# One mixer's value and output-gate products in another order, with their raw weight blocks asked for earlier

## The chip, the core and the metric

The kernel runs on one core of a Trainium2 chip. Its time is the device time of one execution in microseconds (us), the median of several. TensorE (PE) multiplies, VectorE (DVE) and ScalarE (ACT) work element by element, GpSimd (POOL) does a few element-wise pieces and issues the transfers that add what they bring to what is there (accumulating transfers), SyncE (SP) issues the plain loads. Each engine works through its own queue in order: an instruction that waits holds up what stands behind it on that engine.

## What is computed

Two layers of a decoder trunk on 512 tokens of width 1024, in fp32. Each layer is a mixer and a squared-ReLU MLP. The mixer:

```python
h = rmsnorm(x, norm_mix)
z = h @ w_in
splits = [int(s) for s in np.cumsum(IN_WIDTHS)[:-1]]
q_a, k_a, v_a, q_m, k_m, v_m, o_m, if_m, gates = jnp.split(z, splits, axis=-1)
...
att = sliding_window_attention(q_a, k_a, v_a, att_sinks)
...
hm = mlstm_chunkwise(...)
hm = rmsnorm(hm, m_head_norm.reshape(M_HEADS, M_V_DIM)).reshape(B, S, M_V_W)
hm = hm * jax.nn.sigmoid(o_m)
g_a, g_m = jnp.split(gates, 2, axis=-1)
mixed = jax.nn.sigmoid(g_a) * (att @ w_att_branch) + jax.nn.sigmoid(g_m) * (hm @ w_m_branch)
x = x + mixed @ w_out
```

The change concerns the columns `v_m` (values) and `o_m` (output gate) of `h @ w_in`, 512 columns each.

## The kernel before

**Matmuls.** Every fp32 operand is split into a high part (`wh`, a rounded copy made by ACT) and a low part (`wl`, the difference, made by DVE), and every product of tiles is three matmuls of 128x128 by 128x512 (`mm3`). A weight block of 128x512 (256 KB) comes by a plain load from SP into one of three raw buffers, is split into one of four pairs of `wh` and `wl` (`chunk`), and PE uses it for a fixed number of steps. Product banks in PSUM come from five in rotation.

**Order.** `weave` lays a list of PE steps (`fill`, each with a width) in a row and puts the pieces of a second list (`side`) between them where the running width passes their number. So a number such as 24.5 in `side` is a place in the row of PE steps. In one mixer that row is: the mLSTM's q and k (0 to 8), the gates `s0` (8 to 16), the gates `s1`, here called the second gates (16 to 24), product 2 (24 to 26), the two attention projections `a_steps` (26 to 34), the other six products (34 to 46), the gates `s2` and `s3` (46 to 62). Attention's pieces lie in `side` up to about 24, the mLSTM's from 39.6 on.

**Seven products instead of eight.** The tokens are cut in two halves, and so are the 1024 rows of the weights; with the two column groups (output gate and values) there would be eight products of half by half. The kernel computes seven, Strassen's scheme, from sums of weight blocks and sums of token halves. `plan` names for each product the held pair of PSUM banks ("x", "y" or "f"), the half of the activations if no sum is needed, and what is read from the banks at its end: `output` (gate) or `value`. A product in the list `fresh` takes new banks, another one adds onto what its pair holds. Each product has four weight blocks k and two token blocks i, eight steps of one `mm3`; `by_weights` goes through them block by block, `by_tokens` takes two weight blocks for one token block and then for the other.

**Raw blocks.** Products 1 and 2 use plain blocks through `chunk`. The others use `wa[k]` (5, 6, 4) and `wb[k]` (3, 7), each split by `parts_of` (ACT L722, DVE L723): `begin` loads a block by SP (L713) and has POOL add a second one to it (L729); `begin_other` loads `wb[k]`; after the split of product 5, 6 or 3, `more` (L717) has POOL add the block that turns it into the next product's weights. That addition must wait for the split and must land before the next split. The sums of tokens are made by DVE in `sums1`, `sums_next` and `sums3` into a scratch (`sc`), and split (L175, L176).

**What is read at the ends.** `output` copies a bank to SBUF (ACT) the first time and adds to it (DVE L795) the second time; `gates_o` then takes four tanh at 49.1. `value` writes the values `vm`, the first time by ACT (L786), then by DVE (L788). `m_gate` multiplies a head of the mLSTM's output by its gate. `qk_split` splits the mLSTM's q and k, with small copies on POOL (CAST, L676) and low parts on DVE (L679, L682).

Of the kernel before, what the change touches and what calls it, by code (L numbers as in the profile page):

```python
# [16 lines left out]
P = 128  # L17
# [16 lines left out]
def hybrid_kernel(ctx, tc, x, norm_mix, w_in, att_q_norm, att_k_norm, att_sinks, m_gate_bias,  # L34
# [353 lines left out]
    def mixer(l, norm, late, order, phase):  # L388
# [156 lines left out]
        qT, sps, parts = {}, {}, {}  # L545
# [76 lines left out]
        def att_probs(b, kv):  # L622
            sp = sps[b, kv]
            pt = aux()
            for i in range(4):
                pe.transpose(pt[:, i * P:(i + 1) * P], sp[:, i * P:(i + 1) * P], ident)
            hl = split(pt, get=lambda: temp(F32R))
            parts[b, kv] = [(hl, v2[:, 0, max(b - 1, 0), kv])]
            if b > 0:


                own = [temp(F32R) for _ in hl]
                for src, dst in zip(hl, own):
                    s3, d3 = (t.rearrange("p (h q) -> p h q", h=4) for t in (src, dst))
                    gp.affine_select(out=d3, in_=s3, compare_op=ALU.is_ge, fill=0.0, base=0,
                                     pattern=[[0, 4], [1, P]], channel_multiplier=-1)
                parts[b, kv].append((own, v2[:, 1, b - 1, kv]))
# [88 lines left out]
        def begin(k):  # L726
            wa[k] = slot()
            load(wa[k], 0, 0, k)
            gp.dma_start(wa[k], block(0, 1, k), accum_op=ALU.add)  # L729
# [60 lines left out]
        def output(t, i, ps, first):  # L790
            if first:
                so.append(slot() if t else temp())
                sc.activation(so[-1], ps, AF.Copy)
            else:
                ve.tensor_tensor(so[2 * t + i], so[2 * t + i], ps, op=ALU.add)  # L795
# [86 lines left out]
        def m_out(h, t):  # L882
# [11 lines left out]
            if h > 1:  # L894
                m_gate(h, t)

        def m_gate(h, t):
            c = slice(h * MV, (h + 1) * MV)
            ve.scalar_tensor_tensor(hm[t][:, c], so[t][:, c], 1.0, hm[t][:, c], op0=ALU.add, op1=ALU.mult)
# [10 lines left out]

        def a_steps(g, sg):
            def ev_a(m, ps):
                t = sg[m]
                prod.append(t)
                ve.scalar_tensor_tensor(t, t, 1.0, ps, op0=ALU.add, op1=ALU.mult)  # L915

            return feat_steps(att_acts, lambda k: [w_att_branch[l, k * P:(k + 1) * P, 512 * g:512 * g + 512]],
                              ev_a)
# [3 lines left out]
        side += [(27.0, sums1), (31.0, lambda: sums_next(6, 0, 0)), (33.5, lambda: sums_next(3, 0, 1)), (38.0, sums3)]  # L922
# [7 lines left out]
        side.append((49.1, gates_o))  # L930
        side += [(49.3 + 0.9 * h + 0.15 * t, lambda h=h, t=t: m_gate(h, t)) for h in range(2) for t in range(NB)]
# [5 lines left out]
        def head_tr(f):  # L937
            ps = aux()
            for b in range(NB):
# [5 lines left out]
              + vo_steps(5, 1, 3, 6, 7, 4) + s2 + s3, side)  # L945
# [555 lines left out]
```

## Time and profile before

| what | value |
|---|---|
| median of three runs | 1298.05 us (1297.85 to 1299.5) |
| the profiled execution | 1299.13 us |
| its span, first to last instruction | 1297.4 us |
| DVE, ACT, POOL busy | 78%, 60%, 18% of the span |
| HBM read | 182.65 MB |
| products and projections on PE, layer 0 | 137 to 206 us |
| the same in layer 1 | 778 to 849 us |

The terms that the rows use: a row of a timeline is its start and length in us, engine, line, operation, tiles and count, and in brackets the idle time of the engine before it with what ended it. `w` is a raw buffer, `a` a slot (raw blocks, gates, q and k among them), `t` a temporary (sums of tokens among them), `mm` a product bank, `i` the normed activations. Line 47 is the helper of all matmuls, lines 155, 165 and 166 are load, high part and low part of `chunk`, and line 915 is DVE's read of an attention projection's bank. PE's matmuls are pipelined: each row is longer than the distance to the next.

### The profile page before, as it was taken

The page shows a single profiled execution, that of the slowest core. Times are in us where ns is not written, and L with a number is a line of the kernel's source. Part 1 is how long each engine was busy: PE and PEld are TensorE (multiplying, and loading weights), DVE is VectorE, ACT ScalarE, POOL GpSimd, SP SyncE. Part 2 cuts the span into 40 slices and gives each one's busy share as a digit, 9 for nine tenths or more (in the row PEclk, how much of TensorE's full clock was granted, in tenths as well). Part 3 has the DMA queues.
Part 4 walks back from the last instruction along what each step waited for, and adds up shares of the span by engine and source line. Part 5 has one row for each costly group of instructions (what it writes and reads, how often), then busy time and mean ns, then how long its engine had stood idle before and what let it go on. Part 6 is the DMA issues. An engine that isn't in the chain of part 4 may idle for free.

```text
span 1297.4 us, 19218 instructions
## 1 busy us (share of the span) xinstructions
PE 1282.7 (99%) x6930; PEld 1095.2 (84%) x6930; DVE 1008.3 (78%) x1608; ACT 776.3 (60%) x1367; POOL 236.2 (18%) x313
## 2 busy tenths in 40 slices
PE   9999999999999999999999999999999999999998
PEld 6877778888889999999888777788888899999987
DVE  4688898674777897968958888876747879879797
ACT  5568578553465656656554785775435556665563
POOL 4501252000003021131114023310000030311210
PEclk9999999999999999999999999999999999999999
DMA  5422672272369888898224226722714597988953
GB/s 155 111 74 58 187 130 66 74 243 81 98 163 172 240 183 207 199 206 215 33 77 112 66 60 178 129 77 79 259 50 131 146 214 193 205 210 198 217 142 98
DMA packets 135151, 186.01 MB, mean 143 GB/s; under 512 B 10376, under 2 KB 78832, under 8 KB 135056
## 3 DMA queue, kind: packets, MB, share of 16 engines
q1 hardware_dynamic: 94208, 131.82, 33.2%
q0 software_dynamic: 40128, 52.57, 25.5%
q8 instruction: 54, 0.88, 0.3%
q10 hardware_dynamic: 720, 0.40, 0.1%
q14 instruction: 41, 0.34, 0.1%
HBM read 182.65 MB, written 2.10 MB: 142 GB/s over the span
## 4 chain that ended last, share of the span: by engine, by line
PE 91%; DVE 3%; DMA 3%; ACT 2%; issue 1%; DVEq 0%; SPq 0%; ACTq 0%
PE mm L47 73%; PE aux L47 16%; PE aux L52 2%; DMA w<-in_w_in_dram 2%; DMA w<-in_w_att_branch_dram 1%; ACT wh L165 1%; DVE wl L166 1%; ACT t L615 0%; DVE wl L723 0%; DVE t L583 0%; DVE a L915 0%; DMA x<-in_x_dram 0%; DVE t L620 0%; DVE m L609 0%; DVE t L176 0%
## 5 line engine op out<-in xcount | busy, mean ns | idle before, releaser
L47 PE MATMUL mm<-i,wh 128*128 128x512 f32 (+1 forms) x1280 | 353.9, 363 | 0.2
L992 ACT ACTIVATE wh<-raw 128x1024 fp32r<-128x1024 f32 x212 | 223.3, 1056 | 189.4 <-PE mm L47 118.6
L993 DVE TENSOR_TENSOR wl<-raw,wh 128x1024 fp32r<-128x1024 f32 x212 | 255.1, 1219 | 75.3 <-ACT wh L992 75.3
L47 PEld LDWEIGHTS mm<-i,wh 128*128 128x128 f32 x1280 | 222.7, 189 | 30.7 <-DVE a L695 1.1
L47 PE MATMUL mm<-i,wl 128*128 128x512 f32 (+1 forms) x640 | 228.8, 359 | 0.0
L166 DVE TENSOR_TENSOR wl<-w,wh 128x512 fp32r<-128x512 f32 (+1 forms) x192 | 129.0, 675 | 100.7 <-ACT wh L165 96.3
L165 ACT ACTIVATE wh<-w 128x512 fp32r<-128x512 f32 (+1 forms) x192 | 116.7, 610 | 113.8 <-PE mm L47 85.0
L47 PE MATMUL mm<-wh,uh 128*128 128x512 f32 x440 | 171.8, 390 | 0.0
L47 PE MATMUL mm<-wl,uh 128*128 128x512 f32 x440 | 171.7, 390 | 0.0
L47 PE MATMUL mm<-wh,ul 128*128 128x512 f32 x440 | 171.2, 389 | 0.0
L1152 POOL DMA_DIRECT2D raw<-in_w_ff_dram x48 | 62.2, 1303 | 543.0 <-DVE i L179 234.2
L47 PEld LDWEIGHTS mm<-i,wl 128*128 128x128 f32 x640 | 120.9, 189 | 18.5 <-DVE wl L993 0.4
L47 PE MATMUL mm<-wh,i 128*128 128x512 f32 (+1 forms) x352 | 101.3, 361 | 1.2 <-ACT wh L165 0.6
L1038 DVE SCALAR_TENSOR_TENSOR x<-mm,ms,x 128x512 f32<-128x512 f32 x126 | 90.5, 744 | 9.0 <-PE mm L47 8.9
L47 PEld LDWEIGHTS mm<-wh,ul 128*128 128x128 f32 x440 | 82.6, 188 | 17.5
L47 PEld LDWEIGHTS mm<-wh,uh 128*128 128x128 f32 x440 | 82.8, 188 | 16.1
L47 PEld LDWEIGHTS mm<-wl,uh 128*128 128x128 f32 x440 | 82.8, 188 | 15.6
L47 PE MATMUL mm<-a,wh 128*128 128x512 f32 x256 | 79.8, 393 | 2.3 <-DVE a L915 2.3
L47 PE MATMUL mm<-wh,a 128*128 128x512 f32 x256 | 81.4, 393 | 0.0
L47 PEld LDWEIGHTS mm<-wh,i 128*128 128x128 f32 x352 | 62.0, 188 | 12.4 <-DVE i L179 1.5
L1309 POOL DMA_DIRECT2D raw<-in_w_ff_dram x36 | 43.6, 1212 | 149.2 <-DVE wl L993 103.3
L47 PE MATMUL aux<-t,wh 128*128 128x256 f32 x384 | 69.5, 283 | 0.0
(284 smaller groups left out, 2409.3 us busy)
## 6 DMA issues: line engine op xcount, KB each, us to landing
raw<-in_w_ff_dram SPq DMA_DIRECT2D x144, 512.0 KB, 5.1
raw<-in_w_ff_dram POOLq DMA_DIRECT2D x84, 512.0 KB, 7.9
w<-in_w_in_dram SPq DMA_DIRECT2D x112, 256.0 KB, 2.7
a<-in_w_in_dram POOLq DMA_DIRECT2D x32, 256.0 KB, 5.9
w<-in_w_out_dram SPq DMA_DIRECT2D x32, 256.0 KB, 3.1
w<-in_w_att_branch_dram SPq DMA_DIRECT2D x16, 256.0 KB, 5.4
a<-in_w_in_dram SPq DMA_DIRECT2D x16, 256.0 KB, 5.5
w<-in_w_m_branch_dram SPq DMA_DIRECT2D x16, 256.0 KB, 2.7
```

The source lines that it names most:

```text
L47: latest[0] = nc.tensor.matmul(*args, **kw)
L52: latest[0] = nc.tensor.transpose(*args)
L165: sc.activation(wh[:, :off], raw[:, :off], AF.Copy)
L166: ve.tensor_tensor(wl[:, :off], raw[:, :off], f32(wh[:, :off]), op=ALU.subtract)
L992: sc.activation(hi, src, AF.Copy)
L993: ve.tensor_tensor(lo, src, f32(hi), op=ALU.subtract)
L1038: ve.scalar_tensor_tensor(xh[:, cc], ps[i][:, cc], ms[j][:, b:b + 1], xh[:, cc], op0=ALU.mult, op1=ALU.add)
L1152: gp.dma_start(to[h], src(h, i, j), accum_op=ALU.add)
L1309: gp.dma_start(to[h], src(h, i, j), accum_op=ALU.add)
```

## The change

Product 1 goes ahead of product 5, so that the order is 2, the projections, 1, 5, 6, 3, 7, 4. Product 6 follows 5 directly and is the first to write the values of the first token half; 7 follows 3 directly. Product 4 is no longer fresh in banks of its own: it adds onto "x" right behind 7, so that the banks then hold the gate of the second token half whole; ACT takes its tanh straight from PSUM (`output_whole`), and the copy and addition for that half are gone. Product 4 goes by tokens, 6 by weights. The tanh of the first half follows its addition at once, and `gates_o` is gone. The plain loads of `wa` move from 24.5 to 17.0, those of `wb` from 28.0 to 20.0; the first accumulation is a piece of its own at 24.6, tied behind attention's last mask on POOL. Head gates of heads 0 and 1 move forward from 49.3.

```diff
-        qT, sps, parts = {}, {}, {}
+        qT, sps, parts, masked = {}, {}, {}, [None]
...
-                    gp.affine_select(out=d3, in_=s3, compare_op=ALU.is_ge, fill=0.0, base=0,
-                                     pattern=[[0, 4], [1, P]], channel_multiplier=-1)
+                    masked[0] = gp.affine_select(out=d3, in_=s3, compare_op=ALU.is_ge, fill=0.0, base=0,
+                                                 pattern=[[0, 4], [1, P]], channel_multiplier=-1)
...
         def begin(k):
             wa[k] = slot()
             load(wa[k], 0, 0, k)
-            gp.dma_start(wa[k], block(0, 1, k), accum_op=ALU.add)
+
+        def begin_sum(k):
+            with tc.issue_after(masked[0].ins):
+                gp.dma_start(wa[k], block(0, 1, k), accum_op=ALU.add)
...
             if first:
-                so.append(slot() if t else temp())
+                so.append(temp())
                 sc.activation(so[-1], ps, AF.Copy)
             else:
-                ve.tensor_tensor(so[2 * t + i], so[2 * t + i], ps, op=ALU.add)
-
-        def gates_o():
-            for b in range(NB):
-                sc.activation(so[b], so[b], AF.Tanh, scale=half[:, b:b + 1])
-
-        plan = {2: ("f", (0, 1), [(output, 0, True)]), 5: ("y", None, [(value, 1, True)]),
-                1: ("x", (0, 0), [(output, 0, False)]), 3: ("y", None, [(value, 0, True)]),
-                6: ("x", None, [(value, 0, False)]), 7: ("x", None, [(value, 1, False), (output, 1, True)]),
-                4: ("f", (1, 1), [(output, 1, False)])}
+                ve.tensor_tensor(so[i], so[i], ps, op=ALU.add)
+                sc.activation(so[i], so[i], AF.Tanh, scale=half[:, i:i + 1])
+
+        def output_whole(t, i, ps, first):
+            so.append(slot())
+            sc.activation(so[-1], ps, AF.Tanh, scale=half[:, 2 * t + i:2 * t + i + 1])
+
+        plan = {2: ("f", (0, 1), [(output, 0, True)]), 1: ("x", (0, 0), [(output, 0, False)]),
+                5: ("y", None, [(value, 1, True)]), 6: ("x", None, [(value, 0, True)]),
+                3: ("y", None, [(value, 0, False)]), 7: ("x", None, [(value, 1, False)]),
+                4: ("x", (1, 1), [(output_whole, 1, True)])}
...
-            fresh = n in (5, 1, 2, 4) and k == 0
+            fresh = n in (5, 1, 2) and k == 0
...
-                    for n in ns for k, i in (by_tokens if n in (6, 7) else by_weights)]
+                    for n in ns for k, i in (by_tokens if n in (7, 4) else by_weights)]
...
-            if h > 1:
+            if h or t < 2:
                 m_gate(h, t)
...
-        side += [(24.5 + 0.5 * k, lambda k=k: begin(k)) for k in range(4)]
-        side += [(28.0 + 0.5 * k, lambda k=k: begin_other(k)) for k in range(4)]
+        side += [(17.0 + 0.6 * k, lambda k=k: begin(k)) for k in range(4)]
+        side += [(20.0 + 0.6 * k, lambda k=k: begin_other(k)) for k in range(4)]
+        side += [(24.6 + 0.3 * k, lambda k=k: begin_sum(k)) for k in range(4)]
...
-        side.append((49.1, gates_o))
-        side += [(49.3 + 0.9 * h + 0.15 * t, lambda h=h, t=t: m_gate(h, t)) for h in range(2) for t in range(NB)]
+        side += [(46.9 + 0.2 * t, lambda t=t: m_gate(0, t)) for t in (2, 3)]
...
-              + vo_steps(5, 1, 3, 6, 7, 4) + s2 + s3, side)
+              + vo_steps(1, 5, 6, 3, 7, 4)
+              + s2 + s3, side)
```

How this moves instructions, at three places of layer 0. First SP's queue near the end of the second gates. `w` rows are blocks of `chunk`, `a` rows are the raw blocks. Before:

```order
L155 DMA w_343_1642<-in_w_in_dram 128x512
L155 DMA w_349_1674<-in_w_in_dram 128x512
L155 DMA w_358_1706<-in_w_in_dram 128x512
L155 DMA w_365_1735<-in_w_in_dram 128x512
L155 DMA w_369_1750<-in_w_in_dram 128x512
L155 DMA w_374_1785<-in_w_in_dram 128x512
L155 DMA w_381_1805<-in_w_att_branch_dram 128x512
L155 DMA w_393_1839<-in_w_att_branch_dram 128x512
L713 DMA a_364_1732<-in_w_in_dram 128x512
L155 DMA w_397_1859<-in_w_att_branch_dram 128x512
```

And now, from the same block on:

```order
L155 DMA w_351_1658<-in_w_in_dram 128x512
L713 DMA a_289_1408<-in_w_in_dram 128x512
L713 DMA a_301_1452<-in_w_in_dram 128x512
L713 DMA a_309_1487<-in_w_in_dram 128x512
L155 DMA w_357_1690<-in_w_in_dram 128x512
L713 DMA a_317_1519<-in_w_in_dram 128x512
L713 DMA a_328_1574<-in_w_in_dram 128x512
L155 DMA w_366_1722<-in_w_in_dram 128x512
L713 DMA a_337_1604<-in_w_in_dram 128x512
L713 DMA a_344_1632<-in_w_in_dram 128x512
```

The raw blocks stood between blocks of `w_att_branch`; now they stand between the last blocks of the second gates and the first of product 2.

Second, POOL's queue from the splits of q and k on: `a_364` to `a_379` before, and `a_289` to `a_317` now, are `wa[0]` to `wa[3]`; the other `a` tiles are parts of q and k. Before:

```order
L678 MEMSET a_454_2109 64x512
L676 CAST a_453_2106<-a_453_2106 64x512
L717 DMA a_364_1732<-in_w_in_dram 128x512
L717 DMA a_368_1747<-in_w_in_dram 128x512
L676 CAST a_472_2184<-a_472_2184 64x512
L678 MEMSET a_473_2187 64x512
L717 DMA a_373_1782<-in_w_in_dram 128x512
L717 DMA a_379_1801<-in_w_in_dram 128x512
```

And now:

```order
L678 MEMSET a_454_2109 64x512
L676 CAST a_453_2106<-a_453_2106 64x512
L676 CAST a_472_2186<-a_472_2186 64x512
L678 MEMSET a_473_2189 64x512
L678 MEMSET a_504_2330 64x512
L676 CAST a_503_2327<-a_503_2327 64x512
L717 DMA a_289_1408<-in_w_in_dram 128x512
L717 DMA a_301_1452<-in_w_in_dram 128x512
L717 DMA a_309_1487<-in_w_in_dram 128x512
L717 DMA a_317_1519<-in_w_in_dram 128x512
```

The four accumulations behind product 5 have three copies ahead of them instead of one or two, the third of them (`a_503`) from a split that came later before.

Third, DVE's queue while PE is in the first raw product after the projections. `wl` from L166 is a low part of a block of `chunk`, from L723 one of a raw block; `sc` is the scratch of the sums, `t_382` and `t_383` are the gate of the first token half, `mm_432` and `mm_433` the banks "x". Before, where product 5 runs and product 1 is split:

```order
L166 TENSOR_TENSOR wl_449_2085<-w_447_2082,wh_448_2084 128x512
L766 SCALAR_TENSOR_TENSOR sc_388_1827<-sc_388_1827,i_33_274 128x1024
L166 TENSOR_TENSOR wl_452_2097<-w_450_2094,wh_451_2096 128x512
L767 TENSOR_TENSOR sc_388_1827<-sc_388_1827,i_34_275 128x1024
L166 TENSOR_TENSOR wl_457_2115<-w_455_2112,wh_456_2114 128x512
L493 TENSOR_TENSOR cm2_100_592<-t_411_1919,cm2_100_592 4x512
L166 TENSOR_TENSOR wl_460_2127<-w_458_2124,wh_459_2126 128x512
L176 TENSOR_TENSOR t_429_2002<-sc_388_1827,t_428_2001 128x512
```

And now, where product 1 runs and product 5 is split:

```order
L723 TENSOR_TENSOR wl_450_2085<-a_289_1408,wh_449_2084 128x512
L769 SCALAR_TENSOR_TENSOR sc_392_1835<-sc_392_1835,i_33_274 128x1024
L723 TENSOR_TENSOR wl_452_2096<-a_301_1452,wh_451_2095 128x512
L770 TENSOR_TENSOR sc_392_1835<-sc_392_1835,i_34_275 128x1024
L798 TENSOR_TENSOR t_382_1805<-t_382_1805,mm_432_2019 128x512
L798 TENSOR_TENSOR t_383_1810<-t_383_1810,mm_433_2020 128x512
L723 TENSOR_TENSOR wl_456_2113<-a_309_1487,wh_455_2112 128x512
L723 TENSOR_TENSOR wl_458_2124<-a_317_1519,wh_457_2123 128x512
L723 TENSOR_TENSOR wl_467_2154<-a_289_1408,wh_466_2153 128x512
```

The two additions onto the gate, which read product 1's banks, stand between the low parts of blocks 1 and 2 of product 5; the last row is the low part of product 6's block 0. The two reads of product 7's banks "x" keep their place among the low parts of product 4, which then writes to these banks.

More of the change, by code (lines that the diff above doesn't have):

```diff
@@ L893, in m_out @@
             sc.activation(ps[:, :MV], hs, AF.Square, accum_out=hss[:, t, h:h + 1])
-            if h > 1:
+            if h or t < 2:
                 m_gate(h, t)
         def m_gate(h, t):
-            c = slice(h * MV, (h + 1) * MV)
-            ve.scalar_tensor_tensor(hm[t][:, c], so[t][:, c], 1.0, hm[t][:, c], op0=ALU.add, op1=ALU.mult)
+            hs = hm[t][:, h * MV:(h + 1) * MV]
+            ve.scalar_tensor_tensor(hs, so[t][:, h * MV:(h + 1) * MV], 1.0, hs, op0=ALU.add, op1=ALU.mult)
         def m_norm():
@@ L909, in mixer, with ev_a @@
         prod = []
+        def ev_a(t, ps):
+            prod.append(t)
+            ve.scalar_tensor_tensor(t, t, 1.0, ps, op0=ALU.add, op1=ALU.mult)
         def a_steps(g, sg):
[L912 to L915, printed above, removed]
             return feat_steps(att_acts, lambda k: [w_att_branch[l, k * P:(k + 1) * P, 512 * g:512 * g + 512]],
-                              ev_a)
-        side += [(24.5 + 0.5 * k, lambda k=k: begin(k)) for k in range(4)]
-        side += [(28.0 + 0.5 * k, lambda k=k: begin_other(k)) for k in range(4)]
-        side += [(27.0, sums1), (31.0, lambda: sums_next(6, 0, 0)), (33.5, lambda: sums_next(3, 0, 1)), (38.0, sums3)]
+                              lambda m, ps: ev_a(sg[m], ps))
+        side += [(17.0 + 0.6 * k, lambda k=k: begin(k)) for k in range(4)]
+        side += [(20.0 + 0.6 * k, lambda k=k: begin_other(k)) for k in range(4)]
+        side += [(24.6 + 0.3 * k, lambda k=k: begin_sum(k)) for k in range(4)]
+        side += [(27.0, sums1), (31.0, lambda: sums_next(6, 0, 0)), (33.5, lambda: sums_next(3, 0, 1)),
+                 (38.0, sums3)]
         pace = 3.2
```

## The prediction

> **What bounds the kernel now.** I read the page first, then TensorE's (PE's) rows in order of time, then the chain of waits and the table of stretches.
>
> ```profile
> PE 91%; DVE 3%; DMA 3%; ACT 2%; issue 1%; DVEq 0%; SPq 0%; ACTq 0%
> 246.01 9.59 PE mm L47 x42
> ```
>
> PE holds 91% of the chain that ends last; where nothing waits, 42 matmuls take 9.59 us, 0.228 us each. The change leaves their number alone, so it can move only PE's pauses. Between the two attention projections and the seven products stand these (the second row of the fence and the sixth are the ends of the same kind of pause in layers 0 and 1):
>
> ```profile
> 155.20 0.39 PE L47 MATMUL mm<-a,wl 128*128 128x512 f32 x1
> 156.50 0.73 PE L47 MATMUL mm<-a,wh 128*128 128x512 f32 x2 [0.91 <-DVE a L915]
> 168.56 0.50 PE L47 MATMUL mm<-wh,t 128*128 128x512 f32 x1 [0.41 <-DVE a L915]
> 183.04 0.50 PE L47 MATMUL mm<-wl,t 128*128 128x512 f32 x1 [0.47 <-DVE wl L723]
> 183.37 0.63 PE L47 MATMUL mm<-wh,t 128*128 128x512 f32 x2
> 798.67 0.73 PE L47 MATMUL mm<-a,wh 128*128 128x512 f32 x2 [1.40 <-DVE a L915]
> 810.72 0.50 PE L47 MATMUL mm<-wh,t 128*128 128x512 f32 x1 [0.43 <-DVE a L915]
> 821.00 0.50 PE L47 MATMUL mm<-wl,i 128*128 128x512 f32 x1 [0.22 <-DVE wl L166]
> 825.89 0.50 PE L47 MATMUL mm<-wl,t 128*128 128x512 f32 x1 [0.53 <-DVE wl L723]
> ```
>
> A pause costs more than the bracket says. From 155.20 to 156.50 are 1.30 us where 0.23 would do, so 1.07 for a bracket of 0.91; and the first matmul after a pause is followed 0.33 us later (183.04 to 183.37), 0.10 more than usual. I add 0.26 to each bracket. The first pause costs 1.17 and 1.66, sum 2.83. The later ones cost 0.67 and 0.73 in layer 0, and 0.69, 0.48 and 0.79 in layer 1, sum 3.36. All seven: 6.2 us. That is the most that can be won here.
>
> What is behind the first pause, in the chain of waits and in VectorE's (DVE's) rows:
>
> ```profile
> 147.12 7.27 DMA w<-in_w_att_branch_dram
> 154.49 0.64 ACT wh L165
> 155.77 0.69 DVE a L915
> 155.16 0.69 DVE L166 TENSOR_TENSOR wl<-w,wh 128x512 fp32r<-128x512 f32 x1 [1.02 <-ACT wh L165]
> 100.00:135.00 35.00, 34.22 (x165) 26.52 (x164) 30.98 (x79) 29.27 (x87) 7.01 (x11) 1.00 0.23 60
> 135.00:152.00 17.00, 17.00 (x84) 14.10 (x84) 14.93 (x38) 10.47 (x21) 3.53 (x4) 1.00 0.91 237
> 143.80:190.00 46.20, 44.41 (x196) 35.38 (x196) 41.12 (x79) 27.35 (x52) 19.12 (x19) 1.00 0.73 161
> ```
>
> A 256 KB block of w_att_branch took 7.27 us. ACT's copy of it waited, DVE's low part waited for ACT, and behind that low part in DVE's queue stood the bank's evacuation (L915) for which PE waited. The table of stretches (length, then busy time of PE, weight loads, DVE, ACT and POOL, granted clock, DMA share, GB/s) says why: from 135 to 152 us the DMA engines are 0.91 busy, from 100 to 135 only 0.23. In the last stretch DVE is busy 41.1 of 46.2 us: whoever takes away PE's pauses there meets DVE next.
>
> **The loads, moved from the third projection to the second gates.** Per layer eight plain 256 KB loads leave the stretch at 0.91 and enter the one at 0.23. They wait for no buffer, so on SP's queue each costs its issue alone, and the gate blocks behind them have three raw buffers of lead. Four accumulating transfers stay, but on POOL they now find their bases loaded and start when the last mask is through. With 2 MB of the 237 GB/s times 17 us (4 MB) gone, the blocks of w_att_branch should land in time. Gain: the first pause, **-2.83 us**. From below: nothing, if the accumulations alone keep those blocks late.
>
> **The product without sums first.** Its blocks come through the ordinary ring, so neither a sum nor an accumulation is needed for it, and the sums of tokens get one product more of time. The later pauses, **-3.36 us**, are taken away as they stand; what replaces them is the next term.
>
> **What the new order tightens.** Two pairs that shared a raw block with other products between them now follow each other: the sixth product's block is product 5's block plus an accumulation, the seventh's is product 3's. One product is 24 x 0.228 = 5.5 us, and within it must fit the low part, the issue on POOL, the landing and the next split.
>
> ```profile
> a<-in_w_in_dram POOLq DMA_DIRECT2D x1, 256.0 KB, 4.3
> a<-in_w_in_dram POOLq DMA_DIRECT2D x2, 256.0 KB, 5.3
> DMA to landing us min/median/max: 4.1/5.8/6.6
> L722 ACT ACTIVATE wh<-a x40: 615/622/641, 159.1 to 841.8; 128x512 fp32r<-128x512 f32 x40
> 179.22 0.68 DVE L176 TENSOR_TENSOR t<-sc,t 128x512 fp32r<-128x512 f32 x1
> 179.82 0.68 DVE L723 TENSOR_TENSOR wl<-a,wh 128x512 fp32r<-128x512 f32 x1
> 181.10 1.27 DVE L795 TENSOR_TENSOR t<-t,mm 128x512 f32<-128x512 f32 x2
> 166.50 0.69 DVE L682 TENSOR_TENSOR a<-a,a 64x512 fp32r<-64x512 f32 x1
> 198.07 0.28 DVE L868 TENSOR_SCALAR t<-t,bias 128x128 f32<-128x128 f32 x1
> 188.89 0.29 POOL L874 TENSOR_SCALAR_AFFINE_SELECT t<-t 128x128 f32<-128x128 f32 x1
> 189.13 0.86 POOL L717 DMA_DIRECT2D a<-in_w_in_dram  x1
> 167.31 0.39 PE L47 MATMUL mm<-wh,t 128*128 128x512 f32 x1
> 174.02 0.39 PE L47 MATMUL mm<-wh,i 128*128 128x512 f32 x1
> 193.40 0.68 DVE L723 TENSOR_TENSOR wl<-a,wh 128x512 fp32r<-128x512 f32 x1
> 197.41 0.74 DVE L788 SCALAR_TENSOR_TENSOR vm<-mm,minus,vm 128x512 f32<-128x512 f32 x1
> 198.47 0.39 PE L47 MATMUL mm<-wh,i 128*128 128x512 f32 x1
> ```
>
> An accumulation alone lands in 4.3 us, one of a close pair in 5.3, all of L717 within 4.1 to 6.6. A split is 0.62 on ACT and 0.68 on DVE, where one follows the other after 0.60 (179.22 to 179.82). Count from the first matmul of the first raw product (167.31 before). Before, the last product starts at 198.47, that is at 31.16; less the pauses of 0.67 and 0.73, PE alone would be there at **29.8**. In the new order the last product is written onto the bank that the seventh leaves, so it must wait for DVE's read of that bank (L788, now L791). When is that read done?
>
> - The blocks 2 and 3 of product 5 stand on DVE behind the two additions that wait for the first product's end (the third set of queue rows above). Before, the first product ended at 6.0 without its pause (167.31 to 174.02, less 0.67), and so it will now, the read being free at 6.1; the additions take 1.27, two low parts 1.2, and DVE, with a sum of its own just ahead, is some 0.4 late: block 3 is split at 9.0.
> - Its accumulation, 5.0 (between one alone and one of a pair), lands at 14.0. Two reads of product 5's banks stand ahead on ACT (one falls behind the landing, 0.65); with 1.35 for the split block 3 of the sixth product is ready at 16.0. PE wants it at about 11.6 + 4.1 = 15.7, the low part 0.46 later: no pause, or a small one.
> - Ten pieces follow on DVE: four low parts and a sum at 0.60, three splits of q and k at 0.7 (L682 and its like, two of which came later before), two small ones as L868: about 5.5. Block 3 of product 3 is split at 21.5.
> - A mask on POOL, 0.3, then the accumulation, 5.0, and ACT's copy, 0.65: the low part of the seventh product's block 3 starts at 27.5 to 27.7. Before it started at 193.40, 26.1 on this clock.
> - From there to the end of the bank's read were 4.75 us (193.40 to 198.15), 0.66 of them idle; the same rows follow in the same order now: 4.1. The bank is free at 31.6 to 31.8.
>
> So the last product waits 1.8 to 2.0 us in each layer, and I take 2.0: **+4.0 us**. Both landings enter in full: at 4.1 each the wait is 0.2, at 6.6 it is 5.2. I take 5.0, nearer to the single transfer, because in the new order these two transfers have only one issued within a microsecond before them. Below nothing is excluded: an order of work that has nothing to wait for on this bank cannot gain from it.
>
> The Trainium skill, DMA: Bandwidth & Descriptors, section Anatomy of one DMA — SWDGE (gpsimd) path, fits a POOL-issued transfer as 2.0 us plus its bytes at 436 GB/s; for 256 KB that is an estimate of 2.6 us, by which both handovers would be over early and the first rival below would hold. The trace disagrees: no accumulation here landed under 4.1.
>
> The rest costs nothing that PE sees: two additions on DVE and two copies on ACT fewer per layer, four tanh cut in pairs, head gates earlier. In the stretch in which they lie PE has no pause that counts:
>
> ```profile
> 184.00:250.00 66.00, 65.98 (x339) 55.55 (x338) 48.57 (x141) 48.91 (x134) 12.25 (x26) 1.00 0.37 83
> ```
>
> DVE and ACT are busy for three quarters of it, and PE's running matmuls are the cover; without it the eight earlier head gates would be at most some 0.28 each, as the small rows of DVE above.
>
> **Sum.** -2.83 - 3.36 + 4.0 = -2.2 us. On the profiled execution, 1299.13, that is 1296.9; it ran 1.1 over the median of the three, 1298.05, so I forecast **1295.9**.
>
> **Rivals.**
>
> *Short landings.* With accumulations at 4.1 to 4.3, the wait at the last product is 0.2 to 0.6 and the gain 5.0 to 5.8: 1292.3 to 1293.1. For it: fewer plain loads run beside them. Against: all twelve still come within 24 us, and the median was 5.8.
>
> *A starved copy on POOL, slower.* The place is the third CAST of the q/k splits, which now stands ahead of product 5's accumulations.
>
> ```profile
> L676 POOL CAST a<-a x8: 607/740/6094, 160.4 to 847.6; 64x512 fp32r<-64x512 f32 x8
> 163.66 0.14 DVE L477 TENSOR_TENSOR mp<-t,gr 4x1 f32<-4x1 f32 x1
> 165.91 0.55 DVE L477 TENSOR_TENSOR mp<-t,gr 4x1 f32<-4x1 f32 x1
> 167.83 1.87 DVE L915 SCALAR_TENSOR_TENSOR a<-a,mm 128x512 f32<-128x512 f32 x3
> 168.21 0.61 POOL L676 CAST a<-a 64x512 fp32r<-64x512 f32 x1
> ```
>
> A CAST takes 0.61 while DVE reads PSUM (L915), but the one from 160.37 took 6.09, until DVE's L477, 0.14 elsewhere, took 0.55 at 165.91. If the third CAST, due at about 1.7, is held as long, it ends at 7.8; four issues of 0.86 put block 3's at 10.4, not 9.05, and in a burst it lands in 5.9, not 5.0: 2.25 later per layer, 4.5 in all, 1300.4. It decides if the CAST comes after DVE's reads of PSUM, which end at about 2.5. The Trainium skill, SBUF — State Buffer, section Who interferes with whom, says that a DVE instruction with two SBUF inputs keeps out a GpSimd instruction that reads SBUF; the 6.09 and 0.61 agree.
>
> *The projections stay late.* If the four accumulations keep w_att_branch late, the first term falls away: -3.36 + 4.0 = +0.6, 1298.7. For it, the accumulations overlap these blocks; against, half of the bytes are gone.
>
> **How the numbers follow.** Forecast 0.42, short landings 0.20, starved copy 0.20, projections late 0.12, anything else (gate blocks held on SP's queue) 0.06 and slower. A landing 0.6 off moves the two waits by 2.4 in all, so the likeliest case alone spans 1293.5 to 1298.3. The range, 1292.5 to 1301.0, adds the short landings and the starved copy. A change within 0.2%, 2.6 us, cannot be told from none: the bound below is 1295.45. Under it lie the short landings and rather under half of the forecast, 0.39. Over 1300.65 lie most of the starved copy with its upper tail (landings of 6.6 add to it), the rest of the others and a little of the forecast's: 0.26. Between: 0.35.
>
> **What would show it.** Right: w_att_branch landing in under 5 us in both layers, no pause between the projections, a DMA share well under 0.9 in that stretch; then a pause at the last product's first matmul, ended by DVE's read of the bank. Wrong: pauses in the sixth or seventh product ended by a low part (landings longer than I took, or the CAST); a pause at the projections; the accumulations of product 5 issued more than 5 us after the first raw product's start; new pauses in the gate products.

## The result, and the profile after

The changed kernel takes **1304.81 us** (median of five runs, 1303.63 to 1305.84), the kernel before 1298.84 beside it (1297.85 to 1299.5): a ratio of 1.0047, interval 1.0033 to 1.0062. It is 6.0 us slower. The profiled execution took 1304.79 with a span of 1303.1, against 1299.13 and 1297.4 before: 5.7 us more span.

TensorE's rows of the changed kernel that end a pause (and 166.39, the first matmul of the first product behind the projections), first layer 0, then layer 1 (start, length, operation, count, and in brackets the idle time and what ended it). The changed kernel's rows in layer 0 stand about 0.9 us earlier, already well ahead of the change's place, so lengths are to be compared, not positions. "Sixth" and "seventh" product mean products 6 and 7; "the last" is product 4.

```profile
155.57 0.73 PE L47 MATMUL mm<-a,wh 128*128 128x512 f32 x2 [0.47 <-DVE a L917]
166.39 0.39 PE L47 MATMUL mm<-wh,i 128*128 128x512 f32 x1
167.93 0.50 PE L47 MATMUL mm<-wh,i 128*128 128x512 f32 x1 [0.70 <-DVE a L917]
184.00 0.50 PE L47 MATMUL mm<-wl,t 128*128 128x512 f32 x1 [0.31 <-DVE wl L723]
192.13 0.50 PE L47 MATMUL mm<-wh,t 128*128 128x512 f32 x1 [0.54 <-ACT wh L722]
192.85 0.50 PE L47 MATMUL mm<-wl,t 128*128 128x512 f32 x1 [0.23 <-DVE wl L723]
200.99 0.47 PE L47 MATMUL mm<-wh,i 128*128 128x512 f32 x1 [1.08 <-DVE vm L791]
...
790.74 0.73 PE L47 MATMUL mm<-a,wh 128*128 128x512 f32 x2 [0.52 <-ACT t L796]
801.02 0.74 PE L47 MATMUL mm<-a,wh 128*128 128x512 f32 x2 [0.45 <-DVE a L917]
813.37 0.50 PE L47 MATMUL mm<-wh,i 128*128 128x512 f32 x1 [0.69 <-DVE a L917]
829.67 0.49 PE L47 MATMUL mm<-wh,t 128*128 128x512 f32 x1 [0.78 <-ACT wh L722]
838.82 0.50 PE L47 MATMUL mm<-wl,t 128*128 128x512 f32 x1 [0.22 <-DVE wl L723]
846.95 0.47 PE L47 MATMUL mm<-wh,i 128*128 128x512 f32 x1 [1.07 <-DVE vm L791]
```

The pauses at the two projections (`mm<-a`) and at the first product behind them are all still there. New are pauses in the sixth product (184.00, 829.67) and in the seventh (192.13, 192.85, 838.82), ended by a raw block's high or low part, and one at the last product (200.99, 846.95), ended by DVE's read of product 7's bank.

To add them up I take from all of TensorE's rows of these stretches the distance from one row's start to the next, less 0.228 us for each matmul of the first, and count each such excess that is over 0.12 us. It is the **lost time** below, in us over both layers; "first" is the first product behind the projections (5 before, 1 now).

| kernel | projections and first product | other products | last product | sum |
|---|---|---|---|---|
| before | 3.79 | 1.84 | 0 | 5.6 |
| changed | 4.19 | 4.78 | 2.47 | 11.4 |

The difference is 5.8, the span's 5.7. That the two agree so closely is partly luck: ahead of the first projection the changed kernel is 0.9 us earlier, and from there on each layer is 3.4 and 3.2 us longer where the lost time accounts for 2.9. Within these margins the loss is in this place: 0.4 at the projections and the first product, 2.9 in the products between, 2.5 at the last.

Where the lost time in the products comes from, in the rows of ACT, DVE and POOL in layer 0 (L717 is the accumulation that turns a raw block into the next product's):

```profile
175.24 1.88 DVE L723 TENSOR_TENSOR wl<-a,wh 128x512 fp32r<-128x512 f32 x3
176.21 2.63 POOL L717 DMA_DIRECT2D a<-in_w_in_dram  x3 [2.08 <-DVE wl L723]
182.50 1.15 ACT L722 ACTIVATE wh<-a 128x512 fp32r<-128x512 f32 x2 [0.24 <-DMA a<-in_w_in_dram]
183.25 1.29 DVE L723 TENSOR_TENSOR wl<-a,wh 128x512 fp32r<-128x512 f32 x2
184.24 2.67 POOL L717 DMA_DIRECT2D a<-in_w_in_dram  x3 [1.25 <-DVE wl L723]
189.92 0.87 POOL L717 DMA_DIRECT2D a<-in_w_in_dram  x1 [0.87 <-PE mm L47]
191.45 0.63 ACT L722 ACTIVATE wh<-a 128x512 fp32r<-128x512 f32 x1 [2.91 <-DMA a<-in_w_in_dram]
192.11 0.69 DVE L723 TENSOR_TENSOR wl<-a,wh 128x512 fp32r<-128x512 f32 x1 [2.48 <-ACT wh L722]
195.32 1.73 ACT L722 ACTIVATE wh<-a 128x512 fp32r<-128x512 f32 x3 [0.45 <-DMA a<-in_w_in_dram]
196.84 0.68 DVE L723 TENSOR_TENSOR wl<-a,wh 128x512 fp32r<-128x512 f32 x1
200.10 0.74 DVE L791 SCALAR_TENSOR_TENSOR vm<-mm,minus,vm 128x512 f32<-128x512 f32 x1
```

The row at 191.45 is the seventh product's block 0: ACT stood 2.91 us for its accumulation, and DVE 2.48 behind ACT. That accumulation had been second of three in the burst on POOL from 184.24. The rows of DVE that follow, down to the read of the bank at 200.10, are late with it.

At the projections, from the changed kernel's timeline: POOL's first accumulations, ACT's and DVE's rows of the block behind them, the first projection's first matmul, and DVE's first read of its banks.

```profile
133.46 3.61 POOL L732 DMA_DIRECT2D a<-in_w_in_dram  x4
143.98 0.63 ACT L165 ACTIVATE wh<-w 128x512 fp32r<-128x512 f32 x1 [3.71 <-DMA w<-in_w_att_branch_dram]
144.65 0.69 DVE L166 TENSOR_TENSOR wl<-w,wh 128x512 fp32r<-128x512 f32 x1 [2.85 <-ACT wh L165]
142.96 0.62 PE L47 MATMUL mm<-a,wh 128*128 128x512 f32 x2
154.84 2.47 DVE L917 SCALAR_TENSOR_TENSOR a<-a,mm 128x512 f32<-128x512 f32 x4
```

And its table of stretches, with the columns of the prediction; the last two rows are the kernel before, the first of these the stretch from 134 to 144, the other its first projection's first matmul:

```profile
134.00:144.00 10.00, 10.00 (x54) 8.31 (x53) 7.48 (x15) 5.29 (x12) 3.07 (x4) 1.00 0.92 199
135.00:152.00 17.00, 16.87 (x83) 13.65 (x83) 13.77 (x36) 9.78 (x21) 2.07 (x3) 1.00 0.71 172
...
134.00:144.00 10.00, 10.00 (x54) 8.31 (x53) 9.12 (x19) 7.40 (x15) 3.13 (x4) 1.00 0.68 185
...
143.86 0.62 PE L47 MATMUL mm<-a,wh 128*128 128x512 f32 x2
```

The DMA share from 135 to 152 us did fall, from 0.91 to 0.71. But from 134 to 144 it is 0.92, where it had been 0.68: the four accumulations are now issued within 3.61 us, straight ahead of the blocks of w_att_branch. One block kept ACT waiting 3.71 us and DVE 2.85. DVE's first read of the first projection's banks (154.84) comes 11.88 us after that projection's first matmul (142.96); before it was 11.91 (155.77 and 143.86). Nothing was gained.

### The profile page after: what moved, and what is told of

It is laid out like the page before. It is cut to its first block, busy times and chain, and to the rows that moved or that the text cites. A ratio compares the mean times of both kernels' runs of the same rounds, so it can differ in the third digit from the quotient of the medians.

```text
span 1303.1 us, 19216 instructions
## 1 busy us (share of the span) xinstructions
PE 1284.8 (99%) x6930; PEld 1095.5 (84%) x6930; DVE 1008.4 (77%) x1604; ACT 773.7 (59%) x1363; POOL 237.5 (18%) x313
## 5 line engine op out<-in xcount | busy, mean ns | idle before, releaser
L47 PEld LDWEIGHTS mm<-i,wh 128*128 128x128 f32 x1280 | 222.9, 190 | 30.5 <-DVE a L695 1.1
L166 DVE TENSOR_TENSOR wl<-w,wh 128x512 fp32r<-128x512 f32 (+1 forms) x192 | 130.0, 679 | 97.1 <-ACT wh L165 92.3
L47 PEld LDWEIGHTS mm<-wh,ul 128*128 128x128 f32 x440 | 82.7, 188 | 17.5
```

Of the source, the lines that this page charges most:

```text
L47: latest[0] = nc.tensor.matmul(*args, **kw)
L166: ve.tensor_tensor(wl[:, :off], raw[:, :off], f32(wh[:, :off]), op=ALU.subtract)
```

## Experiments

The theory after the result: two separate losses. The handovers from product 5 to 6 and from 3 to 7 are one product apart and too close; what they make late also makes DVE late for the bank of the last product. And the early loads gain nothing because the accumulations behind them come as one burst. The rivals: the shared bank alone is the loss, or the early loads are. Medians and ratios to the kernel before are of runs of both on one chip; the ratios' intervals are 95%.

### 1. No handovers

```diff
             if n == 5:
-                more(wa[k], 1, 1, k)
...
             if n == 3:
-                more(wb[k], 0, 1, k)
```

> The changed kernel without the accumulating transfers behind products 5 and 3: products 6 and 7 take the raw blocks of products 5 and 3 as they are, so their weights are not the right ones; the number of matmuls and of splits stays. Theory (the handovers are too close): the pauses in the sixth and seventh product (2.0 us in layer 0 and 2.7 in layer 1, 4.8 in all, worked out from TensorE's rows of the changed kernel) go, and as the low part of the seventh product's last block comes in time, so does most of the pause at the last product (1.24 and 1.23): 1304.8 less 6.5 to 7.2, about 1298. Rival A (the bank shared by products 7 and 4 alone is the loss): the pause at the last product stays at 1.2 us in each layer and grows by what the others gave up: 1303 to 1305. Rival B (the loss is at the projections, where nothing is changed here): 1304 to 1305, with the pauses in products 6 and 7 passed on to other places.

Measured: 1297.4 us, ratio 0.9983 (0.9975 to 0.9992). Lost time 4.0 at the projections and the first product, none in the other products, none at the last product. Both handovers and the bank go together: the shared bank alone costs nothing when the handovers are gone. This kernel also moves 16 blocks less; experiment 4 takes that rival away, as it leaves none out.

### 2. No read of product 7's banks

```diff
-                3: ("y", None, [(value, 0, False)]), 7: ("x", None, [(value, 1, False)]),
+                3: ("y", None, [(value, 0, False)]), 7: ("x", None, []),
```

> The changed kernel without DVE's two reads of product 7's banks into the values, so the values of the second token half lack one term; product 4 then waits only for the matmuls of product 7. Theory: the pause at the last product (1.24 and 1.23 us) goes and the others stay, 1302.3, a little less if DVE's 1.5 us per layer count elsewhere. Rival A (the bank is the whole loss): 1298 to 1299. Rival B (what is late is the block of product 4 or DVE as a whole, and the read only stood last in the row): 1304 to 1305, the pause staying with another name behind it.

Measured: 1302.66 us, ratio 1.0025 (1.0016 to 1.0033). The pause at the last product is gone, the products between still lose 4.4 us. The bank is the smaller part, as the theory says.

### 3. The first accumulations held back

```diff
         def begin_sum(k):
-            with tc.issue_after(masked[0].ins):
+            seen = sm([1, 1], "seen", 1)
+            done = gp.tensor_copy(seen, prod[k][0:1, 0:1])
+            with tc.issue_after(done.ins):
                 gp.dma_start(wa[k], block(0, 1, k), accum_op=ALU.add)
...
-        side += [(24.6 + 0.3 * k, lambda k=k: begin_sum(k)) for k in range(4)]
+        side += [(31.0 + 0.3 * k, lambda k=k: begin_sum(k)) for k in range(4)]
```

> The changed kernel with the four accumulations of product 5's blocks held on POOL until DVE has read the first projection's banks (a copy of one element per block ties them), instead of issued in one burst behind the last mask. Theory (the burst keeps the first blocks of w_att_branch late, and ACT, DVE and the bank reads behind them): the pause of 0.29 us in the first projection in layer 0 and of 0.68 in layer 1 goes, and part of those at the second projection (0.76 and 0.75) and at product 1 (0.86 and 0.85): 1 to 3 us less, 1302 to 1304. Rival (the bank reads alone, DVE's queue being full, set these pauses): within 0.5 us of the changed kernel, 1304.3 to 1305.3.

Measured: 1300.21 us, ratio 1.0010 (1.0001 to 1.0019), more gain than either theory expected. Of this kernel the stretch that had a share of 0.92:

```profile
134.00:144.00 10.00, 10.00 (x54) 8.29 (x53) 9.31 (x21) 7.33 (x16) 0.27 (x1) 1.00 0.34 93
```

And from its timeline the first projection's first matmul and DVE's first reads of its banks:

```profile
143.68 0.61 PE L47 MATMUL mm<-a,wh 128*128 128x512 f32 x2
153.41 2.47 DVE L919 SCALAR_TENSOR_TENSOR a<-a,mm 128x512 f32<-128x512 f32 x4
```

The share is 0.34, and DVE reads the first bank 9.73 us after the projection's start instead of 11.88. Not only the pauses in the projections go, the one at product 1 goes too: lost time at both together falls from 4.19 to nothing. DVE's lateness of 2 us had been carried over from the projections to product 1. The products between and the last one still lose 3.45 and 2.49, so about 1.3 of the 4.78 in the products between had come from the projections too.

### 4. The handovers two products apart

```diff
-                5: ("y", None, [(value, 1, True)]), 6: ("x", None, [(value, 0, True)]),
-                3: ("y", None, [(value, 0, False)]), 7: ("x", None, [(value, 1, False)]),
+                5: ("y", None, [(value, 1, True)]), 6: ("x", None, [(value, 0, False)]),
+                3: ("y", None, [(value, 0, True)]), 7: ("x", None, [(value, 1, False)]),
...
-                    for n in ns for k, i in (by_tokens if n in (7, 4) else by_weights)]
+                    for n in ns for k, i in (by_tokens if n in (5, 3, 6, 7, 4) else by_weights)]
...
-              + vo_steps(1, 5, 6, 3, 7, 4)
+              + vo_steps(1, 5, 3, 6, 7, 4)
```

> The changed kernel with the order 1, 5, 3, 6, 7, 4, so that each raw block has one other product between its two uses by 5 and 6 and by 3 and 7; the values of the first half are first written from product 3 and added to from product 6; products 5, 3 and 6 go by tokens because the next product adds onto the same banks. Theory (handovers): the pauses in the sixth and seventh product (4.8 us) go and most of the pause at the last product, 1298 to 1300. Rival A (bank sharing): three pairs of neighbours share banks now, 5 and 3, 6 and 7, 7 and 4, each waiting up to 1.2 us per layer: 1303 to 1309. Rival C (going by tokens asks for two blocks at once and makes the second block late): pauses at each product's second block, 1301 to 1305.

Measured: 1298.0 us, ratio 0.9988 (0.9979 to 0.9996). Lost time 4.0 at the projections and the first product, 0.49 in the products between, 0 at the last, although three pairs of neighbours share banks. With the loads and accumulations left as in the change, the order takes back the loss.

### 5. The changed kernel again

> The changed kernel itself once more, so that it is timed on the same chip as the next three: 1.0047 of the kernel before, 1304 to 1306.5, by every theory.

Measured: 1305.01 us, ratio 1.0043 (1.0029 to 1.0057). Lost time 4.6, 4.4 and 2.5 at the three places, 11.5 in all, against 4.2, 4.8 and 2.5 in the first trace: one entry can differ by 0.4 between two executions of the same kernel.

### 6. Both edits: 3 and 4

> The changed kernel with both edits: the order 1, 5, 3, 6, 7, 4 and product 5's accumulations held until DVE has read the first projection's banks. Theory (two separate losses, the burst at the projections and the close handovers): 1298.0 of the order alone less its pauses at the projections and at product 1 (1.95 and 2.33 us from TensorE's rows) gives 1293.7, between 1293 and 1295. Rival (they are not separate: accumulations held back come into the way of the handovers, or of product 5 itself): new pauses in products 5, 3 or 6, 1296 to 1300.

Measured: **1293.27 us**, ratio 0.9951 (0.9939 to 0.9964), faster than both kernels. Its chain of waits through the projections and the first product (start, length, engine and line, matmuls) has nothing but PE in it; its two longest pieces:

```profile
141.84 13.83 PE mm L47 x60
...
156.11 13.65 PE mm L47 x60
```

Sixty matmuls take 13.65 us, 0.228 each: no pause. Lost time is 0, 0.48 and 0. And yet its accumulations take longer to land. The view of one line, L717, with who waited for it and how long its transfers took, of this kernel:

```profile
who waited for it (us, times):
...
DMA to landing us min/median/max: 4.2/6.2/7.3
```

And of the changed kernel:

```profile
who waited for it (us, times):
  ACT wh L722: 11.0, 11
...
DMA to landing us min/median/max: 4.1/5.3/7.1
```

With a median landing of 6.2 nobody waits; in the changed kernel, with 5.3, ACT waits 11.0 us. So it is the distance between the two uses of a block that decides here, not the length of the landing.

### 7. The early loads alone

The kernel before, with `begin`, `begin_sum` and `begin_other` of the change at 17.0, 24.6 and 20.0.

> The kernel before with only the raw loads and the first accumulations moved as in the change; order, plan and products as before. Theory (the burst of accumulations takes the place of the loads in the way of w_att_branch, so this part gains nothing): the pauses at the projections stay near 3.8 us in the two layers, 1298.5 to 1300.5, the same as the kernel before. Rival (my prediction's first term: this part alone is worth the first pause of 1.07 and 1.56): 1295.5 to 1297. Rival (the early loads harm what runs beside them): over 1301.

Measured: 1299.37 us, ratio 0.9999 (0.9990 to 1.0007). This part alone changes nothing. Its chain of waits says why:

```profile
137.29 7.22 DMA w<-in_w_att_branch_dram
144.62 0.64 ACT wh L165
145.28 0.69 DVE wl L166
146.78 1.22 DVE sc L762
```

A block of w_att_branch takes 7.22 us beside the accumulations, where it had taken 7.27 beside the plain raw loads and the accumulations. Another block, the same delay.

### 8. The new order alone

The changed kernel, with the loads and accumulations at 24.5 and 28.0, as before.

> The changed kernel with the raw loads and accumulations asked for where they were before; order and plan as changed. Theory: the pauses of the handovers and of the last product stay at 6.5 to 7.5 us in the two layers and those at the projections at 3.5 to 4.5, so 1304 to 1306, the same as the changed kernel: the whole loss lies in the order. Rival (the early loads have a share in the loss, since loads and accumulations meet the gates and the projections): 1300 to 1303.

Measured: 1305.38 us, ratio 1.0044 (1.0031 to 1.0056): the loss of the whole change. Lost time 6.1 at the projections and the first product, 1.6 over the most that was expected, 3.7 in the products between, 2.5 at the last. The excess is in layer 1, at the second projection (4.0 us); why it is there, and why the time does not show all of it, stays open.

### 9 and 10. One handover at a time

As experiment 1, with only product 5's `more` left out (9) and only product 3's (10).

> The changed kernel without the accumulating transfers behind product 5 alone, so products 6 and 4 have weights that lack a block; those behind product 3 stay. Theory (each handover is too close by itself: a low part of 0.68, an issue of 0.86, a landing of 5.3 at the median and a split of 1.28 make 8.1 us where one product gives 5.5): the pauses in the sixth product (0.6 and 1.2 us) go, those in the seventh and at the last product (2.0 to 2.7 us in each layer) stay at 1.5 or more in each layer: 1300 to 1303. Rival (the first handover is the cause, the second only inherits its lateness): hardly a pause in the seventh product, 1297 to 1299.

> The changed kernel without the accumulating transfers behind product 3 alone, so product 7 has weights that lack a block; those behind product 5 stay. Theory: the pauses in the sixth product stay (0.6 to 1.2 us in each layer), those in the seventh and at the last product go, 1304.8 less about 5: 1299 to 1301. Rival (the bank is held by DVE's late queue whatever the seventh product's blocks do): the pause at the last product stays at 1.2 us in each layer, 1302 to 1303.

Measured: 1300.47 us, ratio 1.0009 (1.0000 to 1.0017), and 1299.6 us, ratio 1.0001 (0.9992 to 1.0009). TensorE's pauses in the products of layer 0, without the first handover:

```profile
192.20 0.50 PE L47 MATMUL mm<-wl,t 128*128 128x512 f32 x1 [0.23 <-DVE wl L723]
200.35 0.47 PE L47 MATMUL mm<-wh,i 128*128 128x512 f32 x1 [1.07 <-DVE vm L789]
```

And without the second:

```profile
183.54 0.50 PE L47 MATMUL mm<-wh,t 128*128 128x512 f32 x1 [0.25 <-ACT wh L722]
184.27 0.50 PE L47 MATMUL mm<-wl,t 128*128 128x512 f32 x1 [0.23 <-DVE wl L723]
```

Without the first, the seventh and the last product still lose 2.1 and 1.5 us in the two layers; without the second, the sixth loses 1.1 and 1.3, and the seventh and the last nothing. So each handover is too close by itself, and the pause at the last product hangs on the second alone.

### 11. Both edits, products 5, 3 and 6 by weights

```diff
-                    for n in ns for k, i in (by_tokens if n in (5, 3, 6, 7, 4) else by_weights)]
+                    for n in ns for k, i in (by_tokens if n in (7, 4) else by_weights)]
```

> The kernel with both edits (1293.27), but products 5, 3 and 6 go by weights again. Then product 3 begins on a bank 0.68 us after product 5's last matmul on it, where ACT's read takes some 0.65, and product 7 so behind DVE's read of product 6's bank of 0.74; by tokens there were 1.37 us. Theory (the read of a shared bank costs what does not fit into this distance): pauses of 0.3 to 1.2 us at the first matmuls of products 3 and 7 in each layer, 1294.5 to 1297. Rival (the readers are never late, so the order within a product does not matter): 1293 to 1294.

Measured: 1295.4 us, ratio 0.9966 (0.9954 to 0.9978). In its layer 0:

```profile
178.17 0.50 PE L47 MATMUL mm<-wh,t 128*128 128x512 f32 x1 [0.46 <-ACT vm L791]
191.42 0.47 PE L47 MATMUL mm<-wh,t 128*128 128x512 f32 x1 [0.49 <-ACT t L867]
```

The first is the start of product 3 behind ACT's read of product 5's bank, as expected. The second is the start of product 7. The row names a copy of ACT's for the mLSTM (L867), which ended last, at 191.33; but DVE's first read of product 6's bank (L793) ended only 0.05 before, at 191.28, and a wait for DVE in PE's queue was released at 191.29. Product 7's first matmul writes that bank. In layer 1 the two end at 831.50 (DVE) and 831.53 (ACT), before the matmul at 831.64. So this pause too is the shared bank, as expected; that copy could add at most 0.05 us. Both pauses come once in each layer. Against experiment 6 this kernel is 2.1 us slower; its lost time is 2.1, of it 1.24 at product 3 and 0.88 at product 7, against 0.48 in experiment 6.

### 12. Two apart, with the loads where they were

Experiment 4 on top of experiment 8.

> The order 1, 5, 3, 6, 7, 4 with the raw loads and the first accumulations asked for where they were before (the run with both edits, 1293.27, but without the early loads and the held accumulations). Theory (the early loads are worth something once the burst behind them is out of the way): the pauses at the projections and at product 1 come back as in the run with the changed order alone, 2.3 to 4.0 us in each layer, so 1297.5 to 1300. Rival (the order alone makes the gain, and the projections catch up by themselves): 1293 to 1295.

Measured: 1297.85 us, ratio 0.9988 (0.9979 to 0.9997). Lost time 5.9 at the projections and the first product, 0.5 in the products between, 0 at the last. That is 0.8 more than in the kernel before, though the span of this trace, 1296.7, is 0.7 less: 1.5 us lie outside what the lost time counts, and stay open.

Together, in us (kernels of one row or column are not all from one chip; the kernel before went from 1298.8 to 1299.6 in these comparisons):

| first accumulations and loads | order before | changed order | 1, 5, 3, 6, 7, 4 |
|---|---|---|---|
| loads where they were | 1298.8 | 1305.4 | 1297.9 |
| early, in a burst (the change) | 1299.4 | 1305.0 | 1298.0 |
| early, accumulations held | not tried | 1300.2 | 1293.3 |

In every row the changed order is 5.6 to 7.5 us over its neighbours; the burst is within 0.6 of the old loads in every column; holding the accumulations takes 4.7 to 4.8 off in both columns where it was tried.

## Why the prediction was wrong

I forecast 1295.9 with a range to 1301.0; it became 1304.8. Term by term:

**The first pause (-2.83 forecast).** The loads left the stretch and its DMA share fell, as I said; the pause stayed. At the projections alone the lost time went from 2.63 to 2.48. The step that failed is "With 2 MB of the 237 GB/s times 17 us (4 MB) gone, the blocks of w_att_branch should land in time". I counted bytes over 17 us. Before, each accumulation waited for its own plain load, so that the four were spread; with the loads done early, only the last mask held them, and all four went out in 3.61 us straight ahead of those blocks. I had written the consequence down ("they now find their bases loaded and start when the last mask is through") and priced it only as a bound and a rival, "The projections stay late", at 0.12. Experiments 3 and 7 show that it was the case.

**The later pauses (-3.36 forecast).** Those inside the products before (1.84 of lost time) did go or were replaced. The two at the first product did not: 0.57 and 0.59 became 0.86 and 0.85. The step was that a product without a sum and an accumulation has nothing to wait for there. But what held PE was DVE's read of a projection's bank, as the row at 168.56 in the prediction says, and DVE was late since the projections: in experiment 3, with the burst away, both pauses are gone. Of the 3.36, about 1.3 was won.

**What the new order tightens (+4.0 forecast).** The mechanism was the right one, the adjacent handovers and the bank of the last product, but the term was too small and sat in one place only. It measured 7.25: 2.47 at the bank, where I had put all 4.0, and 4.78 in the sixth and seventh product, where I had "no pause, or a small one" for the sixth and nothing for the seventh. With 0.15 won at the projections and 1.3 at the later pauses, the three terms measured add up to the 5.8. On the clock of the prediction (from the first matmul of the first product, at 166.39 now), in layer 0:

| step | forecast | measured | row |
|---|---|---|---|
| product 5's block 3 split | 9.0 | 10.1 | DVE's second low part from 175.24, ends at 176.5 |
| its accumulation landed | 14.0 | 16.1 | ACT free to copy at 182.50 |
| low part of the sixth product's block 3 | 16.0 | 17.5 | DVE's first from 183.25, ends at 183.9 |
| product 3's block 3 split | 21.5 | 23.2 | DVE's row at 188.93, ends 189.6 |
| low part of the seventh product's block 3 begins | 27.5 to 27.7 | 30.5 | 196.84 |
| last product begins | 31.6 to 31.8 | 34.6 | 200.99 |

The first 1.1 us is DVE, late from the projections: I had it on time. Of the next 1.0, 0.3 is POOL's queue (product 5's blocks 2 and 3 and the next product's block 0 are issued as three in a row from 176.21, block 3 at 176.81), and ACT could copy it 5.7 us after its issue instead of 5.0. The next two rows win 0.4 back. The rest, 1.2, comes before the low part of the seventh product's block 3: its accumulation was through 0.4 later than I took (ACT's row at 195.32), and 0.9 went to DVE's two reads of product 3's banks, which stood ahead of that low part in DVE's queue. They were late because DVE had stood behind the seventh product's blocks 0 to 2: I followed block 3 alone, and did not ask when block 0 comes. The accumulation for block 0 stood on POOL behind the last one for product 4 (184.24, three in a row), came into a burst, and ACT waited 2.91 us for it: 6.6 us lie between its issue at 184.84 and ACT's row at 191.45. In order, ACT, DVE and PE all stood behind a block that my chain did not contain; PE's pause at 192.13 is this wait.

**The landings.** With a median of 5.3 the landing was near the 5.0 that I took. The two landings of my chain came some 0.7 and 0.4 later than that, about 1.1 of the 2.9 us by which the last product is late; the rest is not their length. Nor did the range add up what it could: its upper case of 6.6 alone would have made 5.2 us of wait in each layer, 6.4 over both layers above what I took, and no gain at the projections another 2.8, together 1305.1.

**The rivals.** *Short landings* did not happen (median 5.3). *A starved copy on POOL* did not happen: the third copy took 0.61, from 167.84. I had named as its mark that product 5's first accumulation goes out more than 5 us after the first product's start. It did, at 171.54, 5.15 after, but behind a low part of DVE's (170.59) that was late: the mark does not tell the two apart. *The projections stay late* happened; the time that I gave it, 1298.7, lacked what the handovers cost.

## What to carry to other kernels

When a raw block is turned in place into the next product's, follow every block of the handover through its split, its issue, its landing and the next split, the first as well as the last, and count products between the two uses: one product (5.5 us) was too little here, two were enough even with landings of 6.2 us at the median. When a load is moved earlier, ask what had been waiting for it: those instructions now start together, and may land on the very transfers that the move was to protect. What is late on an in-order engine at one stage shows as a pause stages later: here holding back the burst cleared the pauses at the projections and, some 12 us later, the one at product 1 as well.

## What the runs showed of the hardware

A copy of one element on POOL can stand as long as one of 64x512. These are POOL's rows in experiment 3, the four small copies that hold the accumulations, and DVE's row at the start of the last:

```profile
154.15 0.18 POOL L732 COPY seen<-a 1x1 f32<-1x1 f32 x1 [19.88 <-DVE a L919]
155.05 0.33 POOL L732 COPY seen<-a 1x1 f32<-1x1 f32 x1
155.91 1.21 POOL L732 COPY seen<-a 1x1 f32<-1x1 f32 x1
157.61 6.06 POOL L732 COPY seen<-a 1x1 f32<-1x1 f32 x1
157.40 1.19 DVE L771 SCALAR_TENSOR_TENSOR sc<-sc,i 128x1024 f32<-128x1024 f32 x1
163.55 0.14 DVE L477 TENSOR_TENSOR mp<-t,gr 4x1 f32<-4x1 f32 x1
```

Three took 0.18 to 1.21 us, the fourth 6.06, from the start of DVE's sums until just after L477 at 163.55. In the kernel before a CAST of 64x512 took 6.09, so one element was no help. In these 6 us DVE ran twelve instructions in a row, all but the two scans (L474) with two inputs in SBUF. The Trainium skill, SBUF — State Buffer, section Who interferes with whom, says that a DVE instruction with two SBUF inputs contends with a GpSimd instruction that reads SBUF; these rows agree, and suggest that a chain of such instructions can hold out a single element for all of its length. In experiment 3 the accumulation behind that copy went out at 163.61 and nobody waited for it. Product 1 stands ahead of product 5 there; what it would cost in an order without that cover was not tried.
